# Branch projections and w_out of an encoder layer as seven block products

## The chip, the cores and the metric

The kernel runs on one core of a Trainium2 chip. The metric is the device time of one execution in microseconds, as the median of several runs. The engines are TensorE (PE, with PEld for its weight loads), VectorE (DVE), ScalarE (ACT), GpSimd (POOL) and SyncE (SP). SP and ACT issue the DMAs.

## The reference

One layer of a streaming encoder for two requests that share their weights: 1024 prompt tokens and 64 sample tokens, which the kernel handles as T = 1088 columns. All is float32.

```python
D_MODEL, SB_HEADS, LRU_WIDTH, MEM_HEADS, FFN_HIDDEN = 1024, 8, 1024, 4, 2816
def layer(x, ...):
    proj = rms_norm(x, norm_mix_g) @ w_in             # q,k,v | x_lru,g_lru | q_mem | gates
    o_sb  = stick_breaking_attention(q_sb, k_all, v_all, q_pos, k_pos)
    o_lru = rg_lru(causal_conv(x_lru, ...), ...) * gelu(g_lru)
    o_mem = softmax(qm @ mem_k.T / 16) @ mem_v        # QK-normed, 4 heads of 256
    g = sigmoid(gates + b_merge)                      # three gates for each channel
    merged = (g[0] * (o_sb @ w_br_sb) + g[1] * (o_lru @ w_br_lru) + g[2] * (o_mem @ w_br_mem))
    x = x + merged @ w_out
    xn2 = rms_norm(x, norm_ffn_g)
    return x + (silu(xn2 @ w_ffn_gate) * (xn2 @ w_ffn_up)) @ w_ffn_down
```

Beside the two outputs, new keys and values, the conv and LRU states and the memory's keys and values are returned.

## The kernel before

Activations are held transposed: 128 channels on the partitions, the 1088 tokens along the free axis, eight such tiles for 1024 channels. Every float32 matrix product is made of three matmuls on halves of the numbers (`mm3`): `split` makes a high part (a cast on ACT, line 72) and a low part (source less high part on DVE, line 73), and high x high, high x low and low x high are accumulated in PSUM.

The stages follow one another: stick-breaking attention (to about 571 us), the recurrent branch with the memory keys (to about 1006), memory attention with the gate logits (to about 1242), the rest of the last head with the first tiles of branch 0 (to 1291), the branches (to 1545), w_out (to about 1670), the FFN's gate and up products (to about 2150), the down product. The three mixers write their outputs to scratch in HBM (`o_scr`, one 128x1088 tile for each 128 channels, stored in pieces `ot` and `omt` as they are made), and the gate logits likewise (`g_scr`).

A branch (`branch`, evacuated by its `ev`, lines 922 to 940) loads eight tiles of `o_scr` on SP's queue (`ob`, line 918), splits them and runs eight tiles of 128 output channels: 8 input tiles x 3 matmuls x 3 column chunks (`CH`: 364, 364, 360), so 72 matmuls. Its evacuation multiplies by the sigmoid of the gate (line 934) and adds on POOL into `mg` (line 935); the third branch splits its results at once into `XM`, w_out's operand. Three tiles of branch 0 fill the last head's attention (`free_a`, `BR_MEM`). w_out runs eight tiles of 72 in the same form, adds the transposed x, squares for the norm on POOL (lines 1072 to 1076), and forms the FFN's operands from each pair of its results (`form_early`), the rest at the end (`form_late`). Weights of these tiles come on ACT's queue (`load_w`).

The FFN's gate and up products already go by `sw_product`: a pair of output tiles and all inputs are cut into 2x2 blocks (weights A11 to A22; inputs B11 to B22 by channel tile and by half of the columns, `HT` = 544), and seven products of block sums (`PAIRS`: A11 x B11, S3 x T3, S2 x T2, A22 x T4, S1 x T1, A12 x B21, S4 x B22) take the place of eight. A product is 24 matmuls of 272 columns (`HC`), for two halves c; a pair is 168. `sw_weights` loads a pair's weights in two halves on SP's queue (r0: A11 and A21, r1: A12 and A22) and forms S1 to S4 on DVE. The products accumulate in three pairs of PSUM banks `bx`, `bw`, `by`: products 1, 3, 5 and 7 in `bx`, 2 and 4 in `bw`, 6 in `by`. `banks4` hands them out in turn from four pairs. ACT copies some partial sums to `swt` (`keep`); DVE evacuates products 4 to 7 (`done`).

Each engine works through its instructions in one fixed order, set when the program is built by a scheduler that goes by the code's order, by dependences and by `tc.high_priority` for the evacuations. A DMA queue issues in that order too.

Of the kernel before, what the change touches and what calls it, by code (L numbers as in the profile page):

```python
# [9 lines left out]
F32 = mybir.dt.float32  # L10
# [39 lines left out]
def kernel(ctx: ExitStack, tc: tile.TileContext, x_prompt, x_sample, mem_prompt, cache_sb_k, cache_sb_v,  # L50
# [40 lines left out]
    BR_MEM = 3  # L91
# [31 lines left out]
    class Bulk:  # L123
# [8 lines left out]
        def steps(self, tiles):  # L132
            w = tiles[0][0]()
            hooks = []
            for i, (_, X, evac, after) in enumerate(tiles):
                wn = tiles[i + 1][0]() if i + 1 < len(tiles) else None
                Xh, Xl = X
                if callable(after):

                    bank, after = after, []  # L140
                    pp = [psm.tile([P, 512], F32, tag="mm", name="mm", bufs=2) for _ in range(2)] + [bank(None)]
                    for k in range(KT):
                        for p, (s, n) in zip(pp, CH):
# [73 lines left out]
    def sw_product(W, X, n, banks, temp, out):  # L217
# [35 lines left out]
        for c in run(6, bx, False):  # L253
            done(0, 1, bx, c, None)
# [28 lines left out]
    def gate_tile(eng=None):  # L283
# [17 lines left out]
    o_scr = [[drm.tile([P, T], F32, name=f"o{b}_{k}") for k in range(KT)] for b in range(3)]  # L301
# [9 lines left out]
    with ExitStack() as c1:  # L311
# [51 lines left out]
        def sb_tiles(h):  # L363
# [6 lines left out]
            def token_rows(src, g, out_p, out_s, to_v):  # L370
# [9 lines left out]
                else:  # L380
                    st = wpl.tile([P, 512], F32, tag="stg", name="kvs", bufs=3)
# [77 lines left out]
        def sb_attn(h):  # L459
            d = heads.pop(h)  # L460
            qh, ql, kh, kl, vh, vl, pv = (d[n] for n in ("qh", "ql", "kh", "kl", "vh", "vl", "pv"))
            es = {}

            def o_out(p, s, n):
                ot = sb.tile([P, 256], F32, tag="ot", name="ot")
                S.copy(ot[:, :n], p[:, :n])
                ST.dma_start(o_scr[0][h][:, s:s + n], ot[:, :n])
# [126 lines left out]
    with ExitStack() as c2:  # L594
# [63 lines left out]
        def mem_out(u, kf):  # L658
# [5 lines left out]
            ko = wpl.tile([P, 512], F32, tag="stg", name="ko", bufs=3).rearrange("p (t d) -> p t d", t=2)  # L664
# [11 lines left out]
        mem_norm()  # L676
        for n in range(KT):
# [43 lines left out]
            graw = wpl.tile([P, 512], F32, tag="stg", name=f"gw{n}", bufs=3)[:, :2 * P]  # L721
# [22 lines left out]
            hh = lp.tile([P, LT], F32, tag="a2", name=f"hh{n}", bufs=1)  # L744
            for gi, (s, m) in enumerate(LSEG):
# [21 lines left out]
    mgp = c4.enter_context(tc.tile_pool(name="mgp", bufs=1))  # L767
    mg = [mgp.tile([P, T], F32, name=f"mg{k}") for k in range(KT)]
    with ExitStack() as c3:
# [32 lines left out]
        def q_tiles(m):  # L802
# [11 lines left out]
            def ev(c, s, n, p):  # L814
# [5 lines left out]
                else:  # L820
                    t = wpl.tile([P, 512], F32, tag="stg", name="sqt", bufs=3)
# [19 lines left out]
        def mem_attn(m, per):  # L841
            d = heads[m]
            pes, pts = {}, {}

# [34 lines left out]
            def mix(g):  # L879
# [26 lines left out]
            mix(4)  # L906
            if m + 1 < MH:
# [3 lines left out]
        def act_tiles(nm):  # L911
            return [[act.tile([P, T], F32R, tag=f"A{x}{k}", name=f"{nm}{x}{k}") for k in range(KT)] for x in "hl"]

        stage = {}

        def load_o(b, k, pool=wpl, tag="raw", bufs=RAWB):
            raw = pool.tile([P, T], F32, tag=tag, name=f"ob{b}{k}", bufs=bufs)
            ST.dma_start(raw, o_scr[b][k])
            return raw

        def load_branch(b, k, X):
            raw = stage.pop(k) if k in stage else load_o(b, k)
            split(X[0][k], X[1][k], raw)

        def branch(b, f, wsrc, X, done=None):
            def ev(ci, s, n, p):
                st = wpl.tile([P, 512], F32, tag="stg", name="sig", bufs=3)
                ST.dma_start(st[:, :n], g_scr[b][f][:, s:s + n])
                S.activation(st[:, :n], st[:, :n], AF.Sigmoid)  # L929
                dst = mg[f][:, s:s + n]  # L930
                if b == 0:
                    V.tensor_mul(dst, st[:, :n], p)
                else:
                    V.tensor_mul(st[:, :n], st[:, :n], p)  # L934
                    G.tensor_add(dst, dst, st[:, :n])  # L935
                if done:
                    split(done[0][f][:, s:s + n], done[1][f][:, s:s + n], dst)
# [329 lines left out]
```

## Time and profile before

| what | us |
|---|---|
| runs | 2428.78, 2433.91, 2435.86 (median 2433.91) |
| profiled execution, its own time | 2429.91 |
| its span | 2427.8 |
| busy: PE, DVE, ACT, POOL | 2361.8, 1191.9, 945.0, 450.9 |
| mean granted TensorE clock | 0.991 |
| branches, 1291 to 1545: length, PE busy | 254.0, 254.0 |
| w_out, 1545 to 1671: length, PE busy | 126.0, 112.5 |
| FFN pairs, 1701 to 2125: length, PE busy | 424.0, 424.0 |

A stage is read by its length against TensorE's busy time and granted clock in it; a line of the waits names the engine that waits, the line and tile of its instruction, and what ended the wait.

### The profile page before, as it was taken

The page shows a single profiled execution, that of the slowest core. Times are in us where ns is not written, and L with a number is a line of the kernel's source. Part 1 is how long each engine was busy: PE and PEld are TensorE (multiplying, and loading weights), DVE is VectorE, ACT ScalarE, POOL GpSimd, SP SyncE. Part 2 cuts the span into 40 slices and gives each one's busy share as a digit, 9 for nine tenths or more (in the row PEclk, how much of TensorE's full clock was granted, in tenths as well). Part 3 has the DMA queues.
Part 4 walks back from the last instruction along what each step waited for, and adds up shares of the span by engine and source line. Part 5 has one row for each costly group of instructions (what it writes and reads, how often), then busy time and mean ns, then how long its engine had stood idle before and what let it go on. Part 6 is the DMA issues. An engine that isn't in the chain of part 4 may idle for free.

```text
span 2427.8 us, 37941 instructions
## 1 busy us (share of the span) xinstructions
PE 2361.8 (97%) x15558; PEld 2313.5 (95%) x15558; DVE 1191.9 (49%) x1989; ACT 945.0 (39%) x1708; POOL 450.9 (19%) x514
## 2 busy tenths in 40 slices
PE   7999999999999999999999999997999999999999
PEld 7899999989999999999989999996999999999998
DVE  4666666665554554334444323345665666562322
ACT  4555555553534433323354323334333333431111
POOL 3222222220211211101000122242222222210000
PEclk9999999999999999999999999998999999999999
DMA  5111111113232232322345443232222222381222
GB/s 158 60 53 53 56 57 57 57 61 94 93 98 87 93 105 70 90 94 84 103 131 171 137 120 90 88 92 63 79 82 72 82 71 85 105 282 44 69 58 63
DMA packets 267012, 218.71 MB, mean 90 GB/s; under 512 B 13891, under 2 KB 253718, under 8 KB 266838
## 3 DMA queue, kind: packets, MB, share of 16 engines
q1 hardware_dynamic: 102744, 131.00, 16.7%
q10 hardware_dynamic: 164094, 85.29, 12.1%
q8 instruction: 122, 2.00, 0.3%
q14 instruction: 52, 0.43, 0.1%
HBM read 157.30 MB, written 58.95 MB: 89 GB/s over the span
## 4 chain that ended last, share of the span: by engine, by line
PE 72%; DMA 2%; DVE 2%; ACT 1%; POOL 1%; issue 1%; ACTq 0%; DVEq 0%; POOLq 0%; SPq 0%
PE sw L226 18%; PE mm L101 16%; PE mm L102 16%; PE mm L103 16%; PE mmk L101 1%; PE mmk L103 1%; PE mmk L102 1%; PE ytp L1223 0%; PE avm L101 0%; PE ptp L868 0%; PE sc L103 0%; PE sc L102 0%; PE sc L101 0%; PE gt L101 0%; PE gt L103 0%
## 5 line engine op out<-in xcount | busy, mean ns | idle before, releaser
L1212 DVE TENSOR_TENSOR y<-y,mm 128x364 f32<-128x364 f32 (+1 forms) x72 | 38.2, 531 | 177.5 <-PE mm L103 174.9
L1170 POOL TENSOR_TENSOR u<-u,R 128x272 f32<-128x272 f32 x66 | 69.6, 1057 | 185.2 <-DVE u L1169 185.2
L935 POOL TENSOR_TENSOR mg<-mg,sig 128x364 f32<-128x364 f32 (+1 forms) x48 | 46.2, 966 | 284.5 <-DVE sig L934 284.5
L453 DVE TENSOR_TENSOR_SCAN e<-ones,e 128x128 f32<-128x128 f32 (+3 forms) x64 | 97.1, 1526 | 0.8
L232 ACT COPY swt<-sw 128x272 f32<-128x272 f32 x132 | 50.9, 387 | 108.4 <-PE sw L226 94.8
L289 DVE TENSOR_SCALAR gst<-mm,prm 128x364 f32<-128x364 f32 (+1 forms) x71 | 41.9, 591 | 103.8 <-PE mm L103 103.8
L452 DVE SCALAR_TENSOR_TENSOR e<-z,e 128x384 f32<-128x384 f32 (+4 forms) x96 | 50.4, 552 | 61.3 <-ACT e L450 57.7
L1154 POOL TENSOR_TENSOR sil<-sil,R 128x272 f32<-128x272 f32 x66 | 53.2, 808 | 146.7 <-DVE sil L1153 143.6
L929 ACT ACTIVATE sig<-sig 128x364 f32<-128x364 f32 (+1 forms) x72 | 35.6, 505 | 112.4 <-DMA sig<-g 107.9
L457 ACT ACTIVATE e<-e 128x128 f32<-128x128 f32 (+3 forms) x64 | 43.8, 685 | 60.1 <-DVE e L456 52.3
L1155 ACT ACTIVATE sil<-sil 128x272 f32<-128x272 f32 x88 | 37.5, 431 | 69.5 <-POOL sil L1154 65.8
L1171 DVE TENSOR_TENSOR u<-u,sil 128x272 f32<-128x272 f32 x88 | 39.9, 456 | 45.4 <-POOL u L1170 44.8
L73 DVE TENSOR_TENSOR al<-at,ah 128x128 fp32r<-128x128 f32 (+2 forms) x96 | 51.0, 546 | 20.5 <-ACT ah L72 20.5
L101 PE MATMUL z<-kh,qh 128*128 128x384 f32 (+4 forms) x96 | 36.5, 380 | 14.6 <-DVE e L456 14.6
L448 ACT ACTIVATE e<-z 128x384 f32<-128x384 f32 (+4 forms) x96 | 45.7, 484 | 10.7 <-PE z L103 7.7
L934 DVE TENSOR_TENSOR sig<-sig,mm 128x364 f32<-128x364 f32 (+1 forms) x48 | 25.1, 530 | 49.4 <-PE mm L103 49.3
L456 DVE TENSOR_TENSOR e<-z,e 128x384 f32<-128x384 f32 (+4 forms) x96 | 48.9, 541 | 0.0
L72 ACT CAST ah<-at 128x128 fp32r<-128x128 f32 (+2 forms) x96 | 43.0, 472 | 10.0 <-PE at L506 10.0
L102 PE MATMUL av<-al,vh 128*128 128x256 f32 x160 | 46.7, 292 | 0.1
L101 PE MATMUL av<-ah,vh 128*128 128x256 f32 x160 | 46.3, 290 | 0.4 <-ACT ah L72 0.4
L506 PE MATMUL at<-ident,e 128*128 128x128 f32 x288 | 45.1, 275 | 1.5 <-ACT ah L72 1.1
L740 POOL TENSOR_TENSOR ig<-ig,xc 128x1092 f32<-128x1092 f32 x8 | 20.4, 2554 | 131.4 <-ACT ig L732 131.4
(1787 smaller groups left out, 8553.7 us busy)
## 6 DMA issues: line engine op xcount, KB each, us to landing
ob<-o SPq DMA_DIRECT2D x24, 544.0 KB, 5.0
hid<-u SPq DMA_DIRECT2D x22, 544.0 KB, 2.7
hr<-hid SPq DMA_DIRECT2D x22, 544.0 KB, 5.9
g<-gst SPq DMA_DIRECT2D x48, 182.0 KB, 3.0
sig<-g SPq DMA_DIRECT2D x48, 182.0 KB, 2.5
out_dram<-kvs SPq DMA_DIRECT2D x32, 256.0 KB, 2.2
x<-mg SPq DMA_DIRECT2D x8, 544.0 KB, 2.7
y<-x SPq DMA_DIRECT2D x8, 544.0 KB, 4.9
```

Of the source, the lines that this page charges most:

```text
L73: (l_eng or V).tensor_sub(l, src, f32(h))
L101: TE.matmul(out, lh, rh, start=start, stop=False)
L102: TE.matmul(out, lh, rl, start=False, stop=False)
L103: TE.matmul(out, ll, rh, start=False, stop=stop)
L226: TE.matmul(bank[c][:, :HC], w[:, wj, i], x[:, xj, cs], start=start and i == 0 and j == 0, stop=i == n - 1 and j == 2, skip_group_check=True)
L232: S.copy(tmp[c][:, j], bank[c][:, :HC])
L452: V.scalar_tensor_tensor(ev, z, 0.0, ev, op0=ALU.max, op1=ALU.add)
L453: V.tensor_tensor_scan(e[:, ::-1], ones1[:n].to_broadcast([n, L]), e[:, ::-1], 0.0, op0=ALU.mult, op1=ALU.add)
L456: V.tensor_sub(ev, z, ev)
L935: G.tensor_add(dst, dst, st[:, :n])
L1154: G.tensor_mul(t, t, R[:, s])
L1170: G.tensor_mul(t, t, R[:, s])
```

## The change

The three branches and w_out are run as seven-product pairs too: twelve pairs of 168 matmuls instead of 24 tiles of 72, and four instead of eight. With that, several things move.

- The mixers keep their outputs in SBUF (`o_tile`), and for each two channel tiles `put_branch` stores the seven operands of the block form: three plain blocks, and four sums that POOL forms (T3, T2, T4, T1, 544 columns each). `o_scr` holds operands of 272 KB now. There are twelve such calls.
- `load_operands` loads 28 operands for a branch into 28 places (`UNITS`), in the order of the products, and splits them in place. The next branch's operands take the same places, product by product, as the last pair gives them up.
- The operands of w_out and of the FFN are formed by `form_operands` from eight finished tiles: for each operand with a sum, three of the four channel pairs on POOL and one on DVE.
- Branch 0 no longer fills the last head's attention; the last three gate tiles do.
- The pair weights of the branches and w_out come on SP's queue. `stg` has four buffers instead of three; weight slots go from six to five, their staging tiles likewise down by one; `banks4` cycles three bank pairs instead of four, and w_out's transposes of x use the fourth (`tr`).
- x is loaded for w_out in 512-column pieces through `stg`, and the down product loads its inputs in place.

The core of the diff:

```diff
+    def put_branch(b, i, x0, x1):
+        d = o_scr[b]
+        lo, hi = slice(0, HT), slice(HT, T)
+        for o, src in (("B11", x0[:, lo]), ("B21", x1[:, lo]), ("B22", x1[:, hi])):
+            ST.dma_start(d[o][i], src)
+        t = {o: wpl.tile([P, HT], F32, tag="stg", name=f"o{o}", bufs=4) for o in ("T3", "T2", "T4", "T1")}
+        G.tensor_sub(t["T3"], x1[:, hi], x0[:, hi])
+        G.tensor_add(t["T2"], t["T3"], x0[:, lo])
+        G.tensor_sub(t["T4"], x1[:, lo], t["T2"])
+        G.tensor_sub(t["T1"], x0[:, hi], x0[:, lo])
+        for o in t:
+            ST.dma_start(d[o][i], t[o])
...
+            put_branch(2, m, *om)
...
-        W_PLACES = [(wpl, "wh"), (wpl, "wl"), (wpl, "wh"), (wpl, "wl")] + PB[12:14]
+        W_PLACES = [(wpl, "wh"), (wpl, "wl"), (wpl, "wh"), (wpl, "wl"), SPARE[0]]
...
-            pool, tag = cycle("b", [(psm, "mm"), (ps, "mm"), (ps, "mm"), (ps, "tr")])
+            pool, tag = cycle("b", [(psm, "mm"), (ps, "mm"), (ps, "mm")])
...
+        def load_operands(b):
+            X = {o: [] for _, o in PAIRS}
+            for oi, (_, o) in enumerate(PAIRS):
+                for i in range(NI):
+                    t = operand_at(oi, i, f"x{b}{o}{i}")
+                    ST.dma_start(f32(t[:, 1]), o_scr[b][o][i])
+                    split(t[:, 0], t[:, 1], f32(t[:, 1]))
+                    X[o].append(t)
+            return X
...
+        def form_operands(xs, temps, nm):
...
+                    e = V if i == NI - 1 else G
+                    src = t
+                    if o == "T3":
+                        e.tensor_sub(t, x1[:, HI], x0[:, HI])
+                    elif o == "T2":
+                        e.tensor_add(t, t, x0[:, LO])
+                    elif o == "T4":
+                        e.tensor_sub(t, x1[:, LO], t)
+                    elif o == "T1":
+                        e.tensor_sub(t, x0[:, HI], x0[:, LO])
...
+                    split(w[:, 0], w[:, 1], src)
...
+        def branch_pair(b, j, W, X):
...
+                if add:
+                    V.tensor_add(t, p, t)
+                    G.tensor_mul(t if b else d, t, g)
+                else:
+                    V.tensor_mul(t if b else d, p, g)
+                if b:
+                    G.tensor_add(d, d, t)
+            sw_product(W, X, NI, banks4, temp, out)
...
+        X = load_operands(0)
+        W = pair_weights(w_br_sb, 0, "wb0")
+        for b in range(3):
+            for j in range(NI):
...
+                branch_pair(b, j, W, X)
+                W = Wn
+            if b < 2:
+                X = load_operands(b + 1)
...
+        X = form_operands(mg, [tt[i // 2][:, i % 2] for i in range(NI)], "xm")
...
+                    r = half(f"xr{k}")
...
+                        LD.dma_start(rv, x_prompt[0, g * 512:(g + 1) * 512, k * P:(k + 1) * P]
```

Three places in the engines' orders. First SP's queue at the end of the last head's attention. Before, the whole-tile loads of branch 0 (`ob`) stand among the pieces of the head's output (`omt`) and the gate logits (`gst`):

```order
L918 DMA ob00_12150<-o0_0_126 128x1088 [waits DMAHW4_49,PE_49]
L918 DMA ob01_12152<-o0_1_127 128x1088 [waits DMAHW5_49,PE_49]
L918 DMA ob02_12154<-o0_2_128 128x1088 [waits DMAHW6_49,PE_49]
L290 DMA g2_6_124<-gst_12034 128x364 [waits DMAHW7_49,DVE_49]
L918 DMA ob03_12156<-o0_3_129 128x1088 [waits DMAHW0_49,PE_49]
L895 DMA o2_4_146<-omt_12059 128x256 [waits DMAHW1_49,Activation_49]
L895 DMA o2_5_147<-omt_12059 128x256 [waits DMAHW2_49]
L895 DMA o2_4_146<-omt_12077 128x64 [waits DMAHW3_49,Activation_49]
L895 DMA o2_5_147<-omt_12077 128x64 [waits DMAHW4_49]
L918 DMA ob06_12256<-o0_6_132 128x1088 [waits DMAHW5_49]
L290 DMA g2_6_124<-gst_12119 128x364 [waits DMAHW6_49,DVE_49]
```

Now the stores of the sums (`oT2` to `oT1`) stand ahead of the eleven last operand loads of branch 0, and behind them the second half of its first weights (`wb00r1`):

```order
L301 DMA o2T23_193<-oT2_12605 128x544 [waits DMAHW7_49,Pool_49]
L301 DMA o2T43_197<-oT4_12606 128x544 [waits DMAHW0_49,Pool_49]
L301 DMA o2T13_201<-oT1_12607 128x544 [waits DMAHW1_49,Pool_49]
L994 DMA x0T11_12733<-o0T11_143 128x544 [waits DMAHW2_49]
L994 DMA x0T12_12737<-o0T12_144 128x544 [waits DMAHW3_49]
...
L994 DMA x0B223_12773<-o0B223_153 128x544 [waits DMAHW4_49]
L176 DMA wb00r1_12779<-in_w_br_sb_dram 128x4x256 [waits DMAHW5_49]
```

The loads have moved behind the stores of what the attention makes last, and the weights behind the loads.

Second POOL at the end of the third branch. Before, the last additions into `mg` are followed by w_out's squares:

```order
L935 TENSOR_TENSOR mg7_9650<-mg7_9650,sig_14924 128x364 [waits DVE_49,Pool_49]
L935 TENSOR_TENSOR mg7_9650<-mg7_9650,sig_14956 128x364 [waits DVE_49,Pool_49]
L935 TENSOR_TENSOR mg7_9650<-mg7_9650,sig_14988 128x360 [waits DVE_49,Pool_49]
L1072 TENSOR_TENSOR ssq_15025<-mg0_9643 128x364 [waits DMAHW3_49,DMAHW2_49,DMAHW4_49,DMAHW1_49,DMAHW5_49,DMAHW0_49,DMAHW7_49,DVE_49,Activation_49]
L1072 TENSOR_TENSOR ssq_15025<-mg0_9643 128x364 [waits DVE_49,Activation_49]
L1072 TENSOR_TENSOR ssq_15025<-mg0_9643 128x360 [waits DVE_49,Activation_49]
```

Now the forms of w_out's operands (`tt`, lines 1008 to 1014) stand between the products with the gates (line 1038) and the additions into `mg` (line 1042) of the last pair:

```order
L1042 TENSOR_TENSOR mg4_12628<-mg4_12628,swt_15518 128x272 [waits DVE_49]
L1008 TENSOR_TENSOR tt_15965<-mg5_12629,mg4_12628 128x544 [waits PE_49,Pool_49]
L1008 TENSOR_TENSOR tt_15964<-mg1_12625,mg0_12624 128x544
L1008 TENSOR_TENSOR tt_15964<-mg3_12627,mg2_12626 128x544
L1010 TENSOR_TENSOR tt_15964<-tt_15964,mg0_12624 128x544 [waits DVE_49]
L1010 TENSOR_TENSOR tt_15964<-tt_15964,mg2_12626 128x544 [waits DVE_49]
L1010 TENSOR_TENSOR tt_15965<-tt_15965,mg4_12628 128x544 [waits DVE_49]
L1038 TENSOR_TENSOR swt_15764<-swt_15764,sig10_15748 128x272 [waits DVE_49]
L1042 TENSOR_TENSOR mg7_12631<-mg7_12631,swt_15764 128x272 [waits Pool_49]
L1012 TENSOR_TENSOR tt_15964<-mg1_12625,tt_15964 128x544 [waits DVE_49,Activation_49]
L1012 TENSOR_TENSOR tt_15964<-mg3_12627,tt_15964 128x544 [waits DVE_49,Activation_49]
L1038 TENSOR_TENSOR swt_15765<-swt_15765,sig10_15748 128x272 [waits DVE_49]
```

What moved is that the last additions, which complete `mg6` and `mg7`, now come behind the forms.

Third TensorE where an up pair of the FFN (`fu1`, seventh product, S4) meets the next gate pair (`fg2`, first product, A11); `sw` with its number is a bank. Before, the first product of `fg2` starts on banks for which it waits for nothing:

```order
L226 MATMUL sw_16861<-xgB220_16014,fu1S4_16618 128x272 [waits DVE_49]
L226 MATMUL sw_16861<-xgB220_16014,fu1S4_16618 128x272 x2
L226 MATMUL sw_16861<-xgB221_16025,fu1S4_16618 128x272 x3
L226 MATMUL sw_16861<-xgB222_16036,fu1S4_16618 128x272 x3
L226 MATMUL sw_16861<-xgB223_16047,fu1S4_16618 128x272 x3
L226 MATMUL sw_17099<-xgB110_15248,fg2A11_16833 128x272 x3
L226 MATMUL sw_17099<-xgB111_15494,fg2A11_16833 128x272 x3
L226 MATMUL sw_17099<-xgB112_15740,fg2A11_16833 128x272 x3
L226 MATMUL sw_17099<-xgB113_15988,fg2A11_16833 128x272 x3
```

Now both halves of the first product wait for DVE:

```order
L210 MATMUL sw_18126<-xgB220_17327,fu1S4_17883 128x272 [waits DVE_49]
L210 MATMUL sw_18126<-xgB220_17327,fu1S4_17883 128x272 x2
L210 MATMUL sw_18126<-xgB221_17330,fu1S4_17883 128x272 x3
L210 MATMUL sw_18126<-xgB222_17333,fu1S4_17883 128x272 x3
L210 MATMUL sw_18126<-xgB223_17336,fu1S4_17883 128x272 x3
L210 MATMUL sw_18364<-xgB110_17239,fg2A11_18098 128x272 [waits DVE_49,Activation_49]
L210 MATMUL sw_18364<-xgB110_17239,fg2A11_18098 128x272 x2
L210 MATMUL sw_18364<-xgB111_17242,fg2A11_18098 128x272 x3
L210 MATMUL sw_18364<-xgB112_17245,fg2A11_18098 128x272 x3
L210 MATMUL sw_18364<-xgB113_17248,fg2A11_18098 128x272 x3
```

The waits on the first product are new; its matmuls stand where they stood.

More of the change, by code (lines that the diff above doesn't have):

```diff
@@ L843, in mem_attn @@
             pes, pts = {}, {}
+            om = [o_tile(f"om{m}{c}") for c in range(2)]
             def scores(t):
@@ L909, in mem_attn @@
                 keys(m + 1, "s")
[L911 to L937, printed above, removed]
-            return (lambda: load_w(wsrc[0, :, f * P:(f + 1) * P], f"wb{b}{f}")), X, ev, []
-        X0 = []
-        def free_a(k):
-            if k is None:
-                return ps.tile([P, 512], F32, tag="av", name="mmx", bufs=2)
-            if not X0:
-                X0.extend(act_tiles("x0"))
-            load_branch(0, k, X0)
         tiles = q_tiles(0)
@@ L963 @@
             done = bulk.count
-            if m == MH - 1:
-                for k, tg in enumerate(("qh0", "ql0", "qh1", "ql1")):
-                    stage[k] = load_o(0, k, mp, tg, 2)
-                bulk.run()
-                assert not stage
-                bulk.start([branch(0, f, w_br_sb, X0) for f in range(BR_MEM)])
             mem_attn(m, MEM_STEP)
@@ L973 @@
             elif m == MH - 2:
-                bulk.run(end - 3 * KT - bulk.count)
+                bulk.run(end - 3 * KT * GATES_MEM - bulk.count)
         bulk.run()
@@ L992 @@
[L992 to L1005 removed]
+        NI = KT // 2
@@ L1013, in at @@
         def at(place, name, dt=F32R):
-            return place[0].tile([P, T], dt, tag=place[1], name=name)
-        xg_place = {}
-        for oi, (_, o) in enumerate(PAIRS):
-            for i in range(KT // 2):
-                xg_place[o, i] = (PA + PB)[oi * (KT // 2) + i]
-        XS = {o: [None] * (KT // 2) for _, o in PAIRS}
-        def operand(o, i, src):
-            t = XS[o][i] = at(xg_place[o, i], f"xg{o}{i}").rearrange("p (x n) -> p x n", x=2)
-            split(t[:, 0], t[:, 1], src)
@@ L1138, with ffn_out, out @@
         NH = FFN // P
         U_PLACES = [(mgp, f"mg{k}") for k in (4, 5, 6, 7)]
[L1141 to L1157 removed]
+        def ffn_out(tiles, last):
+            def out(f, hf, c, p, t, add):
+                d = tiles[f][:, piece(hf, c)]
+                r = R[hf][:, c * HC:(c + 1) * HC]
+                if add:
+                    V.tensor_add(d, p, t)
+                    G.tensor_mul(d, d, r)
+                else:
+                    V.tensor_mul(d, p, r)
+                last(f, hf, c, d)
+            return out
@@ L1158, in gate_pair @@
+        def gate_pair(j, W):
+            sil = [at((RAW, SPARE[3])[f], f"sil{j}{f}", F32) for f in range(2)]
+            sw_product(W, XS, NI, banks4, temp,
+                       ffn_out(sil, lambda f, hf, c, d: S.activation(d, d, AF.Silu)))
             return sil
```

346 lines of the change are left out of this document (164 added, 182 removed).

## The prediction

> **What bounds the kernel now.** I read the engine totals first, then a table of stretches cut at the stage borders, then TensorE's waits, then single tiles and short timelines at the places the change touches.
>
> The engine totals, from the page:
>
> ```profile
> PE 2361.8 (97%) x15558; PEld 2313.5 (95%) x15558; DVE 1191.9 (49%) x1989; ACT 945.0 (39%) x1708; POOL 450.9 (19%) x514
> ```
>
> TensorE is busy for 97% of the 2427.8 us span, and every other engine less than half of it. So time is won by fewer matmul columns and lost by every place where TensorE stands. The stretches tell where it stands now (columns: length, then busy time and count of PE, PEld, DVE, ACT, POOL, then granted clock, DMA share, GB/s):
>
> ```profile
> 1232.00:1242.00 10.00, 4.95 (x32) 4.75 (x31) 7.85 (x12) 4.30 (x4) 0.00 (x0) 0.84 0.77 245
> 1242.00:1291.00 49.00, 48.72 (x317) 48.02 (x316) 18.98 (x52) 27.49 (x50) 0.00 (x0) 0.96 0.32 101
> 1291.00:1545.00 254.00, 254.00 (x1534) 253.97 (x1533) 91.40 (x125) 81.11 (x126) 45.26 (x47) 1.00 0.41 123
> 1545.00:1671.00 126.00, 112.46 (x671) 108.91 (x669) 44.29 (x64) 40.43 (x62) 45.42 (x46) 0.93 0.32 96
> 1671.00:1701.00 30.00, 24.49 (x166) 23.70 (x167) 23.84 (x42) 14.56 (x28) 8.00 (x8) 0.89 0.19 55
> 1701.00:2125.00 424.00, 424.00 (x3390) 424.00 (x3390) 254.45 (x466) 160.43 (x349) 110.67 (x121) 1.00 0.26 82
> 2125.00:2157.00 32.00, 27.24 (x185) 26.72 (x184) 23.64 (x30) 13.91 (x18) 6.86 (x6) 0.89 0.82 276
> ```
>
> The branches (1291 to 1545) and the FFN's gate and up pairs (1701 to 2125) run without one gap at full clock. Loss sits at the start of the branches, inside w_out (1545 to 1671) and at the change from w_out to the FFN. The waits there:
>
> ```profile
> PE xtp L1060 <- DMA xr<-in_x_prompt_dram: 6.0, 1, 6.0
> PE mm L101 <- ACT wb00h L72: 5.1, 1, 5.1
> PE mm L101 <- ACT wo7h L72: 4.9, 1, 4.9
> ```
>
> A wait of that length costs more than itself. Start times after the 4.9 us wait (start, duration, instruction):
>
> ```profile
> 1652.46 0.67 PE L101 MATMUL mm<-xmh,wo7h 128*128 128x364 f32 x1 [4.91 <-ACT wo7h L72]
> 1652.92 0.51 PE L102 MATMUL mm<-xml,wo7h 128*128 128x364 f32 x1
> 1653.23 0.51 PE L101 MATMUL mm<-xmh,wo7h 128*128 128x364 f32 x1
> ...
> 1658.66 0.33 PE L101 MATMUL mm<-xmh,wo7h 128*128 128x364 f32 x1
> 1658.83 0.33 PE L102 MATMUL mm<-xml,wo7h 128*128 128x364 f32 x1
> 1658.99 0.33 PE L103 MATMUL mm<-xmh,wo7l 128*128 128x364 f32 x1
> ```
>
> From 1652.5 to 1658.7 the matmuls start 0.31 us apart, then 0.16: half speed for 6.2 us, so 3.1 us lost besides the wait. I add 3 us to every long stall. The Trainium skill ("TensorE: Matmul & The Clock Gate", Part 1) has the clock halved after an idle window of about 3.4 us and freed after about 3.4 us of work, which by it makes 1.7 us; the row is longer, so the trace agrees with the halving and not with the size, and by the page my two new restarts would cost 2.6 us less in all.
>
> **The change part by part.** *Arithmetic.* Matmul starts of a branch tile (72 matmuls) and of a seven-product pair (168):
>
> ```profile
> L101 PE MATMUL mm<-x1h,wb10h x24: 322/327/331, 1353.4 to 1364.8; 128*128 128x364 f32 x16, 128*128 128x360 f32 x8
> L101 PE MATMUL mm<-x1h,wb14h x24: 322/327/329, 1401.0 to 1412.4; 128*128 128x364 f32 x16, 128*128 128x360 f32 x8
> L226 PE MATMUL sw<-xgB,fg1A x48: 282/288/293, 1722.5 to 1740.4; 128*128 128x272 f32 x48
> L226 PE MATMUL sw<-xgB,fg2A x48: 282/288/293, 1764.5 to 1782.4; 128*128 128x272 f32 x48
> ```
>
> Four tiles take 47.6 us, 11.9 each; 1764.5 less 1722.5 is two pairs, 21.0 each, 3.0 for one product of 24. The 24 branch tiles (286) become 12 pairs (252): 34 gained. The eight w_out tiles (95) become four pairs (84): 11 gained. All of it is on the path, since TensorE is.
>
> *The start of branch 0.* From 1232 to 1291 stand 59.0 us, of which TensorE is busy 53.7 and 3.1 of those go to the half clock after the wait for `wb00h`: 50.6 of work (three branch tiles 35.8, the rest attention), 8.4 lost. The three branch tiles no longer fill the last head's attention; gate tiles moved from earlier do, at no cost. Afterwards this chain lies open behind the attention: the last `om` copy on ACT (0.5, a little under the 0.65 of a 544 cast), four POOL sums, then on SP the eleven last operand loads behind the sums' stores, and behind all of them the second half of the first weights; on ACT the cast of S3's weights stands behind the 27th operand cast, and product 2 needs S3. The nearest rows for each:
>
> ```profile
> L740 POOL TENSOR_TENSOR ig<-ig,xc 128x1092 f32<-128x1092 f32 x8 | 20.4, 2554 | 131.4 <-ACT ig L732 131.4
> L935 POOL TENSOR_TENSOR mg<-mg,sig 128x364 f32<-128x364 f32 x32 | 30.9, 968 | 249.9 <-DVE sig L934 249.9
> L72 ACT CAST xgT<-t 128x544 fp32r<-128x544 f32 x16 | 10.2, 647 | 7.9 <-DVE t L1037 5.1 <-DVE t L1033 1.5 <-DVE t L1042 1.1
> L73 DVE TENSOR_TENSOR xgT<-t,xgT 128x544 fp32r<-128x544 f32 x16 | 11.5, 729 | 0.7 <-ACT xgT L72 0.5
> sig<-g SPq DMA_DIRECT2D x48, 182.0 KB, 2.5
> xr<-in_x_prompt_dram ACTq DMA_DIRECT2D x8, 512.0 KB, 4.1
> ```
>
> Between 968 ns at 364 and 2554 at 1092, a POOL form of 544 takes about 1.36 us: 5.4 for the four. The eleven loads are 3.1 MB: at the 276 GB/s of 2125 to 2157 11 us, at its port share of 0.82 made full 9; eleven casts at 0.65 keep up beside them. Then cast and subtraction of S3, 1.3. Together 0.5 + 5.4 + 10 + 2.5 (a first landing) + 1.3 = 19.7, less the 1 us of product 1 left over, plus 3 for the clock: 22 lost, 13.6 more than now. Ends: 16 (loads pass while the sums run) and 28 (sums at the slow price below).
>
> *Borders between branches.* 28 casts and subtractions for the next branch (28 x 0.73 = 20 us of DVE) fall beside a last pair whose own DVE work is about 12 of 21 us (254 of 424 in the FFN's pairs). Loads are released from the first product on, and operands of product k are needed 18 us after their release, so 10 us of backlog mostly fit. The border shows no loss now. I take 3 us for both, ends 0 and 10.
>
> *Branches to w_out.* The trace of before has the split spread over the evacuations, so its 1545 shows nothing of this. Now 12 forms wait on POOL among the last pair's 14 multiplies and adds of 272. A multiply of that size:
>
> ```profile
> 1754.77 0.77 POOL L1170 TENSOR_TENSOR u<-u,R 128x272 f32<-128x272 f32 x1 [11.64 <-DVE u L1169]
> 1756.45 1.28 POOL L1170 TENSOR_TENSOR u<-u,R 128x272 f32<-128x272 f32 x1 [0.91 <-DVE u L1169]
> ```
>
> Counted from the last pair's start, POOL is free at about 3 us; 12 x 1.36 + 14 x 0.77 = 27 follow, so it ends at 30 if nothing slows it, at 47 if all runs at 1.28/0.77. In the middle it ends near 36. The last T3, on DVE, then needs a subtraction, a cast and a subtraction (2.1). TensorE has the pair's 21 us and product 1's 3. Stall 38 - 24 = 14, less 1 us of product 1 that itself waits, plus 3: 16, ends 10 and 27. DVE blocks on that POOL result, with the w_out weights' subtractions queued behind it; they are late by less.
>
> *Inside w_out and on to the FFN.* The transposes of x in w_out:
>
> ```profile
> L1060 PE MATMUL xtp<-ident,xr 128*128 128x128 f32 x61 | 8.9, 292 | 6.0 <-DMA xr<-in_x_prompt_dram 6.0
> ```
>
> From 1545 to 1701 stand 156 us: 95.4 of tiles, 8.9 of transposes, 21.0 of the first pair, 30.7 lost. Afterwards: 16 at the entry; the x pieces (four of 512 columns a pair, from ACT's queue, into two free `stg` buffers, 4.1 us each to landing) about 3 us in each of three later pairs, 9 in all (3 to 15); at the FFN's entry all 28 splits are late where 16 were spread over w_out before, 15 (11 to 20). That is 40, so 9.3 more than now, against 11.3 of arithmetic.
>
> *FFN pairs.* Their arithmetic stays, but `banks4` cycles three bank pairs instead of four. The first product of a pair now writes the banks that the seventh product of the pair before has just filled. Before an up pair's end DVE goes: add, wait for POOL's multiply, multiply, six times in a row:
>
> ```profile
> 1754.26 0.43 DVE L1169 TENSOR_TENSOR u<-sw,swt 128x272 f32<-128x272 f32 x1
> ...
> 1763.92 0.43 DVE L1169 TENSOR_TENSOR u<-sw,swt 128x272 f32<-128x272 f32 x1
> ...
> 1765.62 0.44 DVE L1171 TENSOR_TENSOR u<-u,sil 128x272 f32<-128x272 f32 x1 [0.66 <-POOL u L1170]
> 1765.98 0.43 DVE L1167 TENSOR_TENSOR u<-sw,R 128x272 f32<-128x272 f32 x1
> ```
>
> ```profile
> 1764.52 3.17 PE L226 MATMUL sw<-xgB,fg2A 128*128 128x272 f32 x24
> ```
>
> The six round trips take 1.95 us each where TensorE delivers a half product every 1.5. So the first half of product 7 is read until 1766.41, 1.9 us after the next pair began at 1764.52. With four bank pairs nobody waits for that; with three the next pair's first matmul does. One subtraction fewer stands in DVE's chain afterwards, which saves a slow POOL multiply (0.4 to 0.5): 1.6 a pair, ten pairs, 16 us, ends 10 and 19. A gate pair's second step is on ACT, and DVE is there in time:
>
> ```profile
> 1785.75 0.44 DVE L1151 TENSOR_TENSOR sil<-sw,R 128x272 f32<-128x272 f32 x1 [0.72 <-PE sw L226]
> ```
>
> This read of its last half ends 0.7 us after the next pair's start at 1785.5, and that bank is written only 1.5 us after the start.
>
> *The rest.* `put_branch` adds 48 POOL sums (65 us, in stages where POOL is mostly idle), and its 84 stores and the longer `stg` tenancy could delay a gate or key store: 3 us, ends 0 and 10. The down stage loads in place and later: 0, ends -3 and 3. Fewer weight slots leave 12 us between release and use, where a cast and a subtraction take 1.3: 0.
>
> Sum: -33.8 + 13.6 + 3 - 11.3 + 9.3 + 16 + 3 = -0.2. Against the profiled execution's 2429.91 us that is 2430. The median of the runs, 2433.91, is 0.16% above this execution.
>
> **The rivals.** *Handoffs at their low ends* (faster). If the eleven loads pass beside the sums (-6), POOL runs uncontended (-6), borders and stores are hidden (-6) and the FFN's entry costs what it does now (-4): 2408. For it: DVE's share in 1291 to 1545 is only 36%. Against it: the FFN entry of now, with less to do, still loses 9 us.
>
> *POOL slowed by DVE* (slower). At the entry to w_out every POOL instruction runs beside DVE's subtractions. The row with a subtraction beside it took 1.28 us, the one without 0.77. If all do, the stall there is 27, the four sums at branch 0 take 3 us more and the up pairs keep their 0.4: 2430 + 11 + 3 + 4 = 2448. It decides once POOL's last form ends beyond 46 us of the last pair. The Trainium skill ("GPSIMD Engine Reference", section 8) says that GpSimd shares its SBUF interfaces with VectorE and contends with instructions of two SBUF inputs, as these subtractions are; the two rows agree, and by that rule alone it would be this case.
>
> *No bank wait* (the change's third bank pair costs nothing, since DVE's order gives way): 2430 - 16 = 2414. Against it: the order of DVE in an up pair is as before.
>
> **How the numbers follow.** Forecast, 2420 to 2441: 0.45. Low ends: 0.22. POOL slowed: 0.20. No bank wait: 0.08. Something unforeseen, mostly a new wait in the mixers: 0.05. A measurement of this kernel tells 0.3% (7.3 us) from no change, so faster is below 2426.6 and slower above 2441.2. Of the forecast's 0.45 about 0.11 lie below; with the low ends (0.20) and no bank wait (0.07) faster has 0.38; same 0.37; slower 0.25, from POOL and the unforeseen. The range 2404 to 2452 takes in both rivals' times and a little beyond; the forecast's own is 2420 to 2441.
>
> **What would show it.** Branch pairs 21.0 us apart, and gaps only at borders: a gap near 20 us before the second product of branch 0, ended by ACT's S3 cast; one near 13 before w_out's second product, ended by a T3; waits of about 1.6 us on DVE's up-pair evacuation at ten starts of a gate pair, 42 us becoming 43.6 a round; an FFN entry like now's. I am wrong if the up-pair waits are absent, if the operand loads land before the attention ends, or if a stall turns up inside the branches.

## The result, and the profile after

The changed kernel takes 2506.42 us (median of 4 runs, 2503.84 to 2508.74) against 2433.49 (2428.78 to 2435.86): the ratio is 1.0302, with a 95% interval of 1.0283 to 1.032. It is slower by 73 us, outside the predicted range. The profiled execution took 2503.84 us with a span of 2502.0, against a span of 2427.8.

From the page of the changed kernel, the totals:

```profile
span 2502.0 us, 39574 instructions
PE 2348.4 (94%) x15945; PEld 2289.0 (91%) x15945; DVE 1359.0 (54%) x2248; ACT 1018.4 (41%) x1936; POOL 650.2 (26%) x689
```

TensorE's busy time fell by 13 us only, where the arithmetic took away some 45: what is left of it ran slower (granted clock 0.975 against 0.991), and its idle time rose from 66 to 154 us. POOL works 199 us longer. TensorE's longest waits, over the whole span:

```profile
PE sw L210 <- ACT wb00S L72: 20.1, 1, 20.1
PE mm L100 <- DVE gst L273: 15.9, 8, 5.2
PE sw L210 <- DVE u L1155: 15.6, 10, 2.3
...
PE stp L1125 <- POOL ssq L1100: 9.3, 2, 6.1
PE xtp L1080 <- DMA xr<-in_x_prompt_dram: 9.1, 4, 8.1
PE tt L763 <- POOL tail L755: 8.5, 1, 8.5
```

The first and the third were forecast (18.7 us for S3 of branch 0, ten waits of 1.6 us for the up pairs). The waits for `gst` and `tail` lie in the mixers, where I had foreseen almost nothing. Divided at the same pieces of work, the two executions stand like this (columns as in the prediction; stretches left out are marked). The changed kernel:

```profile
0.00:541.60 541.60, 506.93 (x3209) 470.45 (x3209) 325.58 (x556) 291.97 (x589) 159.91 (x182) 0.99 0.22 69
541.60:584.70 43.10, 39.10 (x236) 37.53 (x237) 24.37 (x54) 13.55 (x26) 10.26 (x19) 0.92 0.27 94
584.70:928.10 343.40, 335.07 (x2090) 331.51 (x2089) 176.54 (x210) 143.94 (x193) 76.65 (x89) 0.99 0.31 98
...
954.90:1063.70 108.80, 95.11 (x583) 94.32 (x581) 35.20 (x61) 34.08 (x56) 18.05 (x14) 0.92 0.27 87
...
1405.20:1495.90 90.70, 86.41 (x672) 85.84 (x673) 66.77 (x105) 48.23 (x96) 51.08 (x52) 0.97 0.56 184
1495.90:1600.70 104.80, 90.47 (x681) 89.17 (x681) 77.28 (x106) 44.60 (x88) 72.77 (x69) 0.94 0.31 101
1600.70:1757.50 156.80, 134.25 (x950) 128.22 (x949) 114.98 (x176) 74.28 (x140) 83.73 (x84) 0.89 0.31 99
1757.50:2151.70 394.20, 380.04 (x3012) 378.34 (x3012) 223.72 (x417) 143.49 (x312) 95.53 (x109) 1.00 0.24 76
```

The same work in the kernel before:

```profile
0.00:536.60 536.60, 506.31 (x3209) 470.44 (x3209) 321.94 (x558) 292.05 (x589) 144.10 (x170) 0.99 0.23 68
536.60:573.10 36.50, 36.47 (x237) 35.45 (x237) 20.44 (x55) 13.98 (x26) 4.96 (x15) 1.00 0.23 74
573.10:904.60 331.50, 329.85 (x2089) 328.58 (x2088) 177.18 (x210) 143.60 (x193) 53.35 (x77) 1.00 0.30 95
...
931.40:1023.60 92.20, 92.20 (x583) 91.97 (x581) 34.73 (x61) 33.87 (x56) 12.97 (x10) 1.00 0.30 91
...
1353.40:1448.70 95.30, 95.30 (x579) 95.30 (x578) 30.13 (x39) 25.32 (x38) 22.08 (x23) 1.00 0.46 138
1448.70:1545.30 96.60, 96.60 (x586) 96.57 (x584) 34.89 (x56) 30.58 (x55) 23.17 (x24) 1.00 0.28 77
1545.30:1701.50 156.20, 137.15 (x838) 132.81 (x837) 68.44 (x104) 55.29 (x91) 53.92 (x53) 0.92 0.29 88
1701.50:2079.90 378.40, 378.40 (x3025) 378.40 (x3025) 228.84 (x419) 141.59 (x309) 99.22 (x109) 1.00 0.25 79
```

The first four rows of each are the mixers, with the same number of matmuls to within one record; the next are branch 1, branch 2, w_out with the first gate pair, and the nine rounds from there.

| stretch | before | after | change | predicted |
|---|---|---|---|---|
| to the start of branch 1 | 1353.4 | 1405.2 | +51.8 | about +5 |
| branch 1 | 95.3 | 90.7 | -4.6 | about -10 |
| branch 2 to the FFN's first up pair | 252.8 | 261.6 | +8.8 | about -12 |
| nine rounds of gate and up | 378.4 | 394.2 | +15.8 | +14 |
| the rest | 347.9 | 350.3 | +2.4 | +2 |

Of the first row's 51.8, 40.1 are lost by the first matmul of the memory attention's second part (`avm`), which starts at 1063.7 us instead of 1023.6. The other 11.7 come from there to branch 1: the rest of the memory attention, the start of branch 0 and its arithmetic.

### The profile page after: what moved, and what is told of

It reads as the page before. It is cut to its first block, busy times and chain, and to the rows that moved or that the text cites. A ratio compares the mean times of both kernels' runs of the same rounds, so it can differ in the third digit from the quotient of the medians.

```text
span 2502.0 us, 39574 instructions
## 1 busy us (share of the span) xinstructions
PE 2348.4 (94%) x15945; PEld 2289.0 (91%) x15945; DVE 1359.0 (54%) x2248; ACT 1018.4 (41%) x1936; POOL 650.2 (26%) x689
## 5 line engine op out<-in xcount | busy, mean ns | idle before, releaser
L216 ACT COPY swt<-sw 128x272 f32<-128x272 f32 x228 | 86.5, 386 | 157.4 <-PE sw L210 131.0
L457 DVE TENSOR_TENSOR_SCAN e<-ones,e 128x128 f32<-128x128 f32 (+3 forms) x64 | 102.3, 1608 | 0.8
L1038 POOL TENSOR_TENSOR swt<-swt,sig 128x272 f32<-128x272 f32 x48 | 50.0, 1042 | 64.3 <-DVE swt L1037 54.6
L1042 POOL TENSOR_TENSOR mg<-mg,swt 128x272 f32<-128x272 f32 x64 | 60.7, 958 | 4.9 <-DVE swt L1040 1.1
L828 POOL TENSOR_TENSOR sq<-sq,sqt 128x364 f32<-128x364 f32 (+1 forms) x12 | 13.6, 1130 | 156.5 <-ACT sqt L827 156.5
L1031 ACT ACTIVATE sig<-sig 128x544 f32<-128x544 f32 x48 | 30.9, 658 | 55.0 <-DMA sig<-g 48.8
L100 PE MATMUL z<-kh,qh 128*128 128x384 f32 (+4 forms) x96 | 36.6, 381 | 14.5 <-DVE e L460 14.5
```

The costliest lines, as they stand in the source:

```text
L100: TE.matmul(out, lh, rh, start=start, stop=False)
L216: S.copy(tmp[c][:, j], bank[c][:, :HC])
L457: V.tensor_tensor_scan(e[:, ::-1], ones1[:n].to_broadcast([n, L]), e[:, ::-1], 0.0, op0=ALU.mult, op1=ALU.add)
L1038: G.tensor_mul(t if b else d, t, g)
L1042: G.tensor_add(d, d, t)
```

## The experiments

A time without a range is one execution; a time with a range is the median of the number of runs given. Single executions are compared with the profiled execution of the changed kernel (2503.84 us), stretch by stretch.

**No sums.** In `put_branch`:

```diff
-        t = {o: wpl.tile([P, HT], F32, tag="stg", name=f"o{o}", bufs=4) for o in ("T3", "T2", "T4", "T1")}
-        G.tensor_sub(t["T3"], x1[:, hi], x0[:, hi])
...
+        for o, src in (("T3", x1[:, hi]), ("T2", x0[:, lo]), ("T4", x1[:, lo]), ("T1", x0[:, hi])):
+            ST.dma_start(d[o][i], src)
```

> Leaves out put_branch's four POOL sums and their stg buffers: each of the four stores takes a plain block instead, so the branches compute with wrong operands; loads, stores and the number of matmuls stay. The mixers (to the end of the memory attention) cost about 44 us more in the changed kernel than before. Buffer theory (the sums hold all four stg buffers until their stores land, and the gate evacuation on DVE waits for one) and POOL theory (the sums themselves delay POOL's other work): time falls by 40 to 50 us, to about 2458, and TensorE's waits for gst (15.9 us) and tail (8.5 us) go. Store theory (84 more stores and the longer life of the output tiles do it): it falls by less than 10.

This kernel leaves out the four sums and stores plain blocks in their places, so its results are not the layer's; loads, stores and matmuls stay as many. It takes 2460.59 us, 43 less. `avm` starts at 1022.5 us, against 1063.7 in the changed kernel and 1023.6 before: up to there the mixers cost nothing more without sums, with all their stores. So the store theory fell. From `avm` to the memory attention's end it takes some 5 us more than before, as the changed kernel does; no run shows why.

**Own buffers for the sums.**

```diff
+        so, nb = so_pool[0]
-        t = {o: wpl.tile([P, HT], F32, tag="stg", name=f"o{o}", bufs=4) for o in ("T3", "T2", "T4", "T1")}
+        t = {o: so.tile([P, HT], F32, tag="so", name=f"o{o}", bufs=nb) for o in ("T3", "T2", "T4", "T1")}
```

> The sums stay on POOL, but lie in buffers of their own (three in the attention and in the recurrent stage, four in the memory attention), so that stg is left to the gates and keys. Buffer theory: nearly all of what leaving the sums out gains, 35 to 45 us, the gst wait falls to about its 1.4 us of before. POOL theory: under 12 us.

> Own buffers on POOL, timed in rounds: 2464 to 2471, 36 us under the changed kernel.

2467.27 us in one execution, then 2469.99 (4 runs, 2469.09 to 2470.39) against 2505.71 for the changed kernel beside it: 36 us less. `avm` starts at 1032.3 us, so 31.4 of them come in the mixers. The waits of the kernel in own buffers from 500 to 1300 us:

```profile
PE sw L210 <- ACT wb00S L72: 9.2, 1, 9.2
PE mtp L653 <- DVE mt L648: 3.1, 2, 2.9
PE mm L100 <- DVE gst L273: 1.4, 1, 1.4
```

`gst` is back at its 1.4 us, `tail` is gone, and even the wait for S3 is 9 us instead of 20. That last gain comes by an order: in this program S3's cast stands on ACT ahead of the last operand casts, at 1275.19 us against 1281.36 for the next of them (in the trace of the four runs). In the mixers the buffers are the cause. How they do it stands in the changed kernel at the end of the recurrent stage. DVE's last step of the recurrence, then POOL, SP, DVE and TensorE there:

```profile
976.61 1.33 DVE L756 TENSOR_TENSOR ol<-gl,hh 128x1024 f32<-128x1024 f32 x2
```

```profile
978.02 1.33 POOL L296 TENSOR_TENSOR oT<-ol,ol 128x544 f32<-128x544 f32 x1 [0.17 <-DVE ol L756]
...
982.12 1.33 POOL L299 TENSOR_TENSOR oT<-ol 128x544 f32<-128x544 f32 x1
```

```profile
979.38 4.42 SPq L301 DMA_DIRECT2D o1T<-oT  x4
```

```profile
981.50 0.69 DVE L671 COPY ko<-mkt 128x512 f32<-128x512 f32 x1 [2.85 <-DMA o1T<-oT]
982.90 0.60 DVE L273 TENSOR_SCALAR gst<-mm,prm 128x364 f32<-128x364 f32 x1 [0.71 <-DMA o1T<-oT]
984.24 0.60 DVE L273 TENSOR_SCALAR gst<-mm,prm 128x364 f32<-128x364 f32 x1 [0.75 <-DMA o1T<-oT]
```

```profile
977.91 0.42 PE L763 MATMUL tt<-ident,tail 128*64 128x128 f32 x1 [8.47 <-POOL tail L755]
983.55 0.67 PE L100 MATMUL mm<-Ah,wg14h 128*128 128x360 f32 x1 [5.22 <-DVE gst L273]
```

The four sums of a `put_branch` take all four `stg` buffers. Buffers are handed out in the code's order, and there this call stands ahead of the key copies (`ko`) and the gate's evacuations (`gst`) on DVE, which want a `stg` buffer too. So these wait for a landing of a sum's store, but before that for the sums, and before those for the recurrence's last step (`ol`), whose result is summed. TensorE stands behind them for its bank: between 969.4 and 983.55 us it runs but one transpose (`tt`). With own buffers the same evacuation runs ahead of that step:

```profile
956.27 0.59 DVE L273 TENSOR_SCALAR gst<-mm,prm 128x364 f32<-128x364 f32 x1
962.18 1.34 DVE L761 TENSOR_TENSOR ol<-gl,hh 128x1024 f32<-128x1024 f32 x2
```

The four buffers instead of three, meant to carry this, are just as many as one call takes. The waits for `gst` and `tail` add to 24.4 us; the rest of the 40 is in part slow matmuls behind them (granted clock 0.92 from 954.9 to 1063.7) and the waits of the next paragraph.

**Sums on DVE.** Own buffers, and `V` for `G` in the four sums.

> The sums of put_branch in own buffers and on DVE instead of POOL, the rest as in the changed kernel. Without the sums at all 7 us less was seen than with them on POOL in own buffers. If those are the time that POOL takes (5.5 us of sums at the end of each stage, before the last stores), DVE's half duration saves 2 to 6 us against own buffers on POOL; if they are VectorE and POOL hindering one another in the attention, where DVE is the busiest engine, it is 0 to 8 us worse.

2471.43 us (4 runs, 2467.4 to 2473.18), the same as with POOL (2469.99), so the sums' own length is not what is left. Some 10 us in the mixers are not given back by own buffers (`avm` at 1032.3 us against 1022.5 without sums). 5.8 of them come in the attention. There the sums push a subtraction of POOL onto two scans of DVE, which take 3.35 us instead of 1.58, and TensorE then waits 1.59; with three such waits POOL and DVE cost 4.8 us by hindering one another there. With own buffers, then without sums:

```profile
194.16 2.41 POOL L73 TENSOR_TENSOR wq3l<-wq3r,wq3h 128x1024 fp32r<-128x1024 f32 x1
194.66 3.35 DVE L461 TENSOR_TENSOR_SCAN e<-ones,e 128x128 f32<-128x128 f32 x2
198.59 0.33 PE L513 MATMUL at<-ident,e 128*128 128x128 f32 x1 [1.59 <-ACT e L465]
```

```profile
192.06 2.40 POOL L73 TENSOR_TENSOR wq3l<-wq3r,wq3h 128x1024 fp32r<-128x1024 f32 x1 [6.80 <-ACT wq3h L72]
194.33 1.58 DVE L452 TENSOR_TENSOR_SCAN e<-ones,e 128x128 f32<-128x128 f32 x2
```

Right behind the attention the next stage's first step waits until the stores of the sums have landed:

```profile
573.81 0.21 ACT L613 ACTIVATE sp<-prm 128x8 f32<-128x8 f32 x1 [7.84 <-DMA o0T<-oT]
```

What this wait on ACT costs TensorE was not tested by itself.

**Four bank pairs.**

```diff
-            pool, tag = cycle("b", [(psm, "mm"), (ps, "mm"), (ps, "mm")])
+            pool, tag = cycle("b", [(psm, "mm"), (ps, "mm"), (ps, "mm"), (ps, "tr")])
```

> Four bank pairs in turn again, the fourth from the buffers of x's transposes, nothing else. Bank theory: the ten waits of 1.6 us for the up pair's evacuation (15.6 us in all) go and a gate and an up pair take 42.1 us again instead of 43.7: 13 to 18 us less; w_out, where the transposes now share banks with the products, within 5 us either way. Rival, that DVE is simply late and the wait moves to the second product: under 5 us.

2492.46 us, 11 less. The waits for the up pairs' evacuation are all gone, and from the first gate pair to the end it is 761.2 us instead of 775.7: the bank theory holds, at 14.5. From branch 2 to there it is 8.5 us longer; 5.9 of this come in branch 2 and 2.6 in w_out, whose transposes now share the fourth pair with the products. Whether that sharing is the cause was not tested. In the changed kernel the wait looked like this (TensorE, then DVE's last evacuations):

```profile
1779.35 3.86 PE L210 MATMUL sw<-xgB,fg1A 128*128 128x272 f32 x20 [2.35 <-DVE u L1155]
```

```profile
1778.77 0.43 DVE L1155 TENSOR_TENSOR u<-sw,R 128x272 f32<-128x272 f32 x1
...
1779.60 0.43 DVE L1155 TENSOR_TENSOR u<-sw,R 128x272 f32<-128x272 f32 x1
```

The gate pair's first product starts 0.15 us after the end of the read of the first half.

**The first weights ahead.**

```diff
-        X = load_operands(0)
-        W = pair_weights(w_br_sb, 0, "wb0")
+        W = sw_weights(w_br_sb[0, :, :2 * P], "wb00", w_slot, first_stage)   # r0 in wx, the others in raw
+        X = load_operands(0)
```

> The weights of branch 0's first pair are issued ahead of its operands, in buffers that are free during the last head's attention (raw), nothing else. Queue theory: product 2 no longer stands behind the 27th operand cast; the 20.1 us wait for S3 goes, and a wait of 2 to 6 us for T1's operands comes before product 5: 13 to 18 us less. Rival, that the operands' loads end the wait anyway: under 5 us less.

2491.14 us, 12.7 less, just under the expected 13. From the attention's last matmul to branch 1 it is 93 us instead of 106. TensorE's waits in the first pair now:

```profile
1300.15 4.79 PE L210 MATMUL sw<-x0T,wb00S 128*128 128x272 f32 x33 [0.38 <-ACT om L899]
1306.07 1.89 PE L210 MATMUL sw<-x0T,wb00S 128*128 128x272 f32 x13 [1.13 <-DVE x0T L73]
1310.38 2.01 PE L210 MATMUL sw<-x0T,wb00A 128*128 128x272 f32 x14 [0.59 <-DVE x0T L73]
```

Nothing waits for S3. The operands come nearly in time: waiting for them costs some 2 us here, so most of the 20.1 us came from the order of the queues.

**Three mends together,** and on top of them two single edits of w_out: its squares on ACT, or its x in whole tiles on SP's queue.

```diff
-                    G.tensor_mul(t, d, d)
+                    S.activation(t, d, AF.Square)
```
```diff
-                        LD.dma_start(rv, x_prompt[0, g * 512:(g + 1) * 512, k * P:(k + 1) * P]
+                r = at(SPARE[2], f"xr{k}", F32)
+                ST.dma_start(rv, x_prompt[0, :, k * P:(k + 1) * P].rearrange("(t p) n -> p t n", p=P))
```

> Three mends together: own buffers for the sums, the first weights ahead, four bank pairs (in the branches and the FFN; three in w_out, where the transposes of x use the fourth). If the three causes are separate their gains add: 36.5 + 12.7 + 14 to 18 off the changed kernel's 2503.8 us, so 2436, between 2430 and 2442, which is still the kernel before or slightly slower. If they share a cause, over 2448.

> The three mends, and w_out's squares for the norm formed on ACT instead of POOL (POOL only adds). POOL-backlog theory: TensorE's waits for ssq before the FFN (9.1 us) fall under 2, 8 to 12 us less than the three mends alone. Rival, that ACT's own copies out of PSUM come later by it: under 3 us less.

> The three mends, and w_out's x loaded on SP's queue into a buffer that is free, instead of on ACT's queue behind the casts of w_out's operands. Queue theory: the 8.2 us wait for x at the start of w_out and the 2 us waits later go, 8 to 14 us less than the three mends alone. Rival, that POOL's forms would have held TensorE there anyway: the wait turns into one for xmB or xmT, under 4 us less.

2440.9, 2435.04 and 2445.97 us. The gains of the three add: 62.9 us, and 2440.9 lies in the expected 2430 to 2442. Both single edits missed. Squares on ACT give 5.9 us of 8 to 12; the wait for `ssq` falls only from 8.8 to 7.1 us, and one of 10.4 for x appears. With x on SP it is 5.1 us longer, where 8 to 14 less were expected. The wait for x that was to go is not in the trace of the three mends, which waits 5.5 us for DVE's `swt` there; with x on SP there are waits of 3.7 us for `xmB`, 6.5 for the copies of x and 5.0 for `swt`. That fits the rival but does not show it: each is one execution, and executions of one kernel lie up to 13 us apart in the last runs.

**All mends,** with half of the operand forms on DVE (`e = V if i >= NI - 2 else G`), then without the move of x, then with product 7's additions into `mg` on DVE:

```diff
-                    G.tensor_add(d, d, t)
+                    (G if add else V).tensor_add(d, d, t)
```

> All mends: the three, squares on ACT, x on SP, and half of the forms of w_out's and the FFN's operands on DVE (two of four channel pairs instead of one). If the losses behind the branches are POOL's, this takes 20 to 32 us off the three mends alone, to 2404 to 2416, below the kernel before. If DVE becomes the bound there, no less than the better of the two single edits.

> All mends but the move of x to SP's queue: the three, squares on ACT, half of the forms on DVE, x in pieces on ACT's queue as in the changed kernel. If x on SP costs what it did alone (5 us), this is 2418; if the forms on DVE free ACT's queue, so that the pieces come in time, as well. If with the forms on DVE the whole-tile load on SP is the better one, it is 2428 or more. Against the three mends with squares on ACT (2435) it shows the forms alone: POOL theory 8 to 16 us less, DVE-bound theory under 3.

> As the run before, and the last additions of a branch pair into mg (product 7, four of its sixteen POOL operations in branches 1 and 2 being the two of each half) are on DVE. POOL-backlog theory: the temporary of product 7 comes free sooner, so TensorE's waits for ACT's first copy (swt, 9 to 10 us) and for w_out's operands shrink, 4 to 10 us less. Rival, that DVE at some 75% there is as late as POOL: no gain, within 2 us, or a loss.

2423.4, 2427.73 and 2426.64 us in one execution each, the kernel before beside them at 2432.2, 2434.26 and 2434.26. The first misses its 2404 to 2416; the second gives 7.3 us off 2435 where 8 to 16 were expected, and leaves open which way of loading x is better, since the first kernel's median below is 2433.57; the third gains 1.1, as its rival had it. With several runs each:

> All mends with x on SP, and the last additions of a branch pair on DVE. If the 1 us that this gave with x on ACT's queue is real it adds to 2423: 2420 to 2424, a ratio to the kernel before of 0.994 to 0.998. If DVE is the bound by then, 2424 to 2430.

> The kernel of all mends again, timed in rounds: 2421 to 2427, a ratio to the kernel before of 0.994 to 0.999, so a small gain of the seven-product form over the kernel before that an interval can tell. If its first look was luck, 2428 to 2436 and no difference.

The kernel of all mends takes 2433.57 us (11 runs, 2429.96 to 2437.4), a ratio of 1.0012 (1.0003 to 1.0021): no gain; its single execution above was 6.6 us under the lowest of the eleven. With the additions on DVE besides it takes 2423.22 (11 runs, 2417.12 to 2429.9), a ratio to before of 0.9969 (0.9959 to 0.998). So the move of two additions in eight is worth 10 us here, and this kernel is 0.3% faster than the kernel before.

**POOL relieved alone.** The changed kernel with w_out's squares on ACT, half of the forms and product 7's additions on DVE, and nothing else.

> The changed kernel with POOL relieved behind the mixers and nothing else: w_out's squares on ACT, half of the operand forms on DVE, the last additions of a branch pair on DVE. From the third branch's start to the FFN's second pair the changed kernel stands 63 us, where the prediction had 40. POOL theory: 12 to 20 us of it go, time 2486 to 2494. Rival (the order of ACT's and SP's queues holds TensorE there, and POOL's share only shows as a wait): under 5 us.

> The changed kernel itself, for the comparison on the same chip: 2500 to 2510.

2491.74 us (2490.74 to 2493.24) against 2505.71 (2501.4 to 2508.16): 14.0 less. The three edits were not timed one by one. Branch 2 takes 101.9 us instead of 105.4, w_out with the first gate pair 143.4 instead of 155.6. POOL's forms and multiplies in the changed kernel (groups of 1250 to 1680 us):

```profile
L1038 POOL TENSOR_TENSOR swt<-swt,sig 128x272 f32<-128x272 f32 x48 | 50.0, 1042 | 64.3 <-DVE swt L1037 54.6 <-ACT x2T L72 9.8
L1010 POOL TENSOR_TENSOR tt<-tt,mg 128x544 f32<-128x544 f32 x3 | 5.2, 1725 | 4.6 <-DVE xmT L73 4.6
L1012 POOL TENSOR_TENSOR tt<-mg,tt 128x544 f32<-128x544 f32 x3 | 4.9, 1654 | 0.0
```

A form takes 1.65 to 1.73 us there, a multiply 1.04; the same form in the recurrent stage, beside a quiet DVE, 1.33.

## Why the prediction was wrong, point by point

- **Arithmetic: right.** Three starts of branch 1's pairs (1428.16, 1449.54 and 1470.66 us) lie 21.4 and 21.1 us apart, for 21.0.
- **Start of branch 0: right, in part by luck.** 20.1 us of waiting for S3, for 18.7, and the 24 matmuls behind it took 5.2 us instead of 3.2: 22 lost, as forecast. The terms partly cancel: the sums took 7.0 us for 5.4 and the casts 7.7 for 10. And most of it was an order: with the weights ahead it went, while leaving the sums out shortened the wait to 16.2 us only. The 3 us for the clock rest on a row read too simply: in the kernel before, the granted clock was 0.50 from 1642 us to 1658.6, over two waits (6.0 us, ended at 1645.3, and then the 4.9), so the slow row is not the doing of the 4.9 us alone. After the 20.1 us wait 2.0 us were lost.
- **Borders between branches: too small.** 3 us forecast; waits of 2.8 and 4.0 us for the evacuation of product 7 came, with 1.6 and 2.2 us lost to slow matmuls right behind them: about 11 us in all, besides smaller waits inside the branches.
- **Branches to w_out, w_out and the FFN's entry: the place right, the size not.** 40 us forecast, 63 stand there (261.6 less 198.3 of work: two times 84.2, 8.9 and 21.0), some of them already in branch 2. The wait that was named, about 13 us for a T3 before w_out's second product, did not come. TensorE waited 8.1 us for x instead: the x pieces of the first pair stand on ACT's queue behind casts that wait for POOL's forms.

```profile
1595.91 0.64 ACT L72 CAST xmT<-tt 128x544 fp32r<-128x544 f32 x1 [1.13 <-POOL tt L1014]
1597.11 0.37 ACTq L1077 DMA_DIRECT2D xr<-in_x_prompt_dram  x1
```

  At the FFN's entry the prediction had 15 us for late splits; the waits of 9.3 us are for the sums of squares on POOL, which it does not name. Relieving POOL took 14 us off the kernel; what makes the rest of the 23 beyond the forecast stays open.
- **FFN pairs: right.** Ten waits, 15.6 us for 16; gone with a fourth bank pair.
- **The rest: the step that failed.** "`put_branch` ... could delay a gate or key store: 3 us, ends 0 and 10." The mixers lost 40.1 us up to `avm`. I counted POOL's time and the stores, and put the longer tenancy of the buffers into 3 us without counting it, though it is in the diff that one call takes all four and that the gate evacuation takes from the same four. Shown: own buffers give 31.4 us of it back, leaving out the sums all of it. The 0.05 for "a new wait in the mixers" names the place and no mechanism.
- **The rivals.** "POOL slowed by DVE" fits the rows of forms behind the branches, 1.65 to 1.73 us for 1.33, but not its own sign: POOL's last addition of the last pair ends some 44 us after the pair's start, later than the forecast's 36 and short of the 46 of the sign. Its 2448 was not enough for the time. "No bank wait" and "Handoffs at their low ends" fell. The Trainium skill ("GPSIMD Engine Reference", section 8) has GpSimd contend with VectorE's instructions of two SBUF inputs; the durations of 1.33 and 1.73 us agree with it.

The sum of the misses, by the table: 47 up to branch 1 (37 of it in the mixers up to `avm`), 5 in branch 1, 21 from branch 2 to the FFN's first up pair, 2 behind it; 75 for the 74 between 2429.7, which the prediction's sum gives, and 2503.8.

## What to carry to other kernels

Where a new step takes buffers from a pool that others use, count how many of them one call holds at once and for how long, from its place in the code's order to the landing of its store, and ask which engine's next instruction wants one: here a producer that took the whole pool stalled the evacuation, and through it TensorE. A change that removes 45 us of matmuls pays only if each handoff it creates has its operands, weights, banks and buffers ready, and each of these has a queue order of its own to look up. Where an engine is nowhere the busiest, look at its load in the last part of each stage, priced by rows in which its neighbours are as busy as they will be there.

## What the runs showed that was not expected

- Shorter waits than 4.9 us slow TensorE as well. After 2.8 us of waiting, 24 matmuls of 272 columns took 4.75 us, after 4.0 us 5.4, where 3.17 is usual. The granted clock was 0.50 in the first 3.2 and 3.4 us behind these two waits:

```profile
1405.19 4.75 PE L210 MATMUL sw<-x1B,wb10A 128*128 128x272 f32 x24 [2.81 <-DVE mg L1040]
1428.16 3.24 PE L210 MATMUL sw<-x1B,wb11A 128*128 128x272 f32 x24 [0.18 <-DVE swt L1040]
```

  The row of 1779.35 above has 2.35 us of waiting, and 20 matmuls in 3.86 us, where 2.7 is usual. Behind eight waits of 1.5 us in the FFN 24 matmuls take 3.23 to 3.24 us at a clock of 1.00. So in this kernel a wait of 2.4 to 4 us cost 1 to 2 us more than it was long. By the Trainium skill ("TensorE: Matmul & The Clock Gate", Part 1) the clock falls after an idle window of about 3.4 us; here it fell behind waits of 2.35 and 2.81 us already.
- The runs of one kernel lie some us apart: 2417 to 2430 for eleven of the best one, 2430 to 2437 for eleven of all mends, 2427 to 2436 for twenty-two of the kernel before. The single execution of all mends, 2423.4 us, lay 10 us under the median of its eleven later ones, so a difference of 5 us between single executions shows nothing.
